# One encoder layer on one core: dense groups of 256 and 272 columns, row sums and squares moved, operands of down loaded ahead, the tail by column groups

## The chip, the core and the metric

The kernel runs on one core of a Trainium2 chip. The metric is the device time of one execution in microseconds (us), the median of three runs. Engines are called as in the profile: PE (TensorE's matmuls), PEld (its weight loads), DVE (VectorE), ACT (ScalarE), POOL (GpSimd) and SP (SyncE, which issues most DMAs here).

## What is computed

One layer of a streaming encoder for 1024 prompt tokens and 32 sample tokens, 1056 columns in all, with a width of 1024 and a hidden width of 4096, in float32:

```
h  = rms_norm(x, ln1_g);   proj = h @ w_in
a  = diff_attention(q, k, v, ...)            # 4 heads, chunk-causal
c  = layer_norm(depthwise_conv(u, w_dw)) ;  c = c * sigmoid(c)
x  = x + concat([a, c]) @ w_out
h2 = rms_norm(x, ln2_g)
x  = x + square(relu(h2 @ w_up)) @ w_down
y  = rms_norm(x, ln_f_g)
```

The other outputs are k, v and the last rows of the convolution's input.

## The kernel before, in words

Tokens are columns: a tile holds 128 features by up to 1056 tokens. Every float32 operand is split into a high part (by ACT, `whi`, `hTh`, `dh`) and a remainder (by DVE or POOL, `wlo`, `hTl`, `dl`), and a product is three matmuls: high by high, low by high, high by low. Instructions stand in the source in one order, and a scheduler arranges each engine's own queue, along which the engine then works.

- **Start and dense blocks** (`x_stat`, `x_group`, `act_groups`, `products`, L101). x is loaded in nine tiles of 128 tokens (the last has 32); `XSET` says which tiles form a set. Per tile, ACT squares and sums it (L262); per set, PE transposes (`pst`), ACT copies (`xT`, L282), DVE scales (`hfx`, L291) and ACT and DVE split into `hTh` (L295) and `hTl` (L296). The blocks of w_in are then multiplied in four groups of columns, `GRP`, 264 each.
- **Out projection** (`part`, then the loop of `pw`, L101). For each of four groups and for the row blocks `ob` 3 to 7, a product is added to x by DVE (L962), and `rows_in` copies x with ln2's gain into the quads `B` (four row blocks of 528 columns), squares it on ACT (L907) and sums the squares on POOL (L908, `ssacc`). Two psum tiles (`psM`) take turns. `b_sums` makes the sums of quads that the up projection needs (`T1`, `T2`, `T4`, L919), for half of the columns at once, all four row blocks.
- **Up projection** (`up_p1`, `up_p2`, `up_steps`). 16 blocks of 256 hidden columns; each is a 2 by 2 block product done with seven products (Strassen-like) from the operands `B00`, `B10` and `X3` to `X7`, the split sums (`to_x`). Five blocks run their first product ahead (`NPRE`), each with one pending psum tile (`psF`, four of two banks). ACT evicts the first product (L1051) and applies relu and square; DVE adds and subtracts (L1067, L1068). The four results and three sums of them go to DRAM (`ud`). `row_stat` makes the mean square of ln2 with a matmul by ones.
- **Down projection** (`u_load`, `u_split`, `d_a`, `w_prep`, `d_run`). Four chunks of the hidden width, each with seven products in the order `PRODS` = 1, 2, 6, 7, 4, 5, 3. A step loads operands two products ahead into pool `act[0]`, splits the next one (`dh` on ACT L876, `dl` on DVE L877), prepares its weights (`w_of` makes sums of them, L1232 to L1235) and adds the result (L1244, or ACT L1281 for the first time). `residual` adds x (kept in DRAM as `x2d`), scaled by `vb` (L1201, L1204), at four places named in `RES`; `row_scales` reads the mean square back for this.
- **Tail** (`final`). Eleven tiles of tokens, `FT`, are transposed back by PE (L1297), squared on ACT (L1302), scaled by DVE (L1303, L1305, L1306) with a power on POOL (L1304), and stored. Five are queued after product 4 of the last chunk, three after half of product 3, three at the end.

## Time and profile before

| | |
|---|---|
| median of three runs | 1224.98 us (1224.97 to 1226.77) |
| the profiled execution | 1224.9 us, its span 1223.1 us |
| mean granted clock | 0.994 |
| PE busy | 1176.2 us, 96% of the span |
| PEld busy | 1131.1 us, 92% |
| DVE busy | 887.9 us, 73% |
| ACT busy | 580.9 us, 47% |
| POOL busy | 142.1 us, 12% |

Busy time is the union of an engine's instructions. A window's row gives, for a stretch of the span, the busy time and number of instructions of each engine and the mean clock that TensorE was granted, as a share of the higher of its levels. A timeline's row gives start, duration, engine, line, operation with the names of its tiles, a count where several are joined, and in brackets how long the engine was idle before and what ended that. Matmuls overlap in the pipeline: one lasts longer than the distance to the next.

### The profile page before, as it was taken

Reading aid. Unit: us, or ns where it says so; the run is one execution under the profiler, and the core shown is the slowest. Engines: PE = TensorE matmul, PEld = TensorE weight load, DVE = VectorE, ACT = ScalarE, POOL = GpSimd, SP = SyncE. Lnnn points to the kernel's source line nnn. Section 1 sums busy time; section 2 is a strip of 40 time slices with the busy share of each in tenths; the row PEclk is TensorE's granted clock in tenths of the full one; section 3 lists DMA queues with packets and bytes.
Section 4 is the critical chain, followed back from the end, with each engine's and each line's share of the span. In section 5 each row is a group of like instructions: output and inputs, shape, how many; then the busy total and the mean of one; then the engine's idle time right before and its main releaser. Section 6 shows DMA issues by size and latency. Waiting matters only on the chain. (4 is left out here: it accounts for less than half of the span.)

```text
span 1223.1 us, 23089 instructions
## 1 busy us (share of the span) xinstructions
PE 1176.2 (96%) x9340; PEld 1131.1 (92%) x9340; DVE 887.9 (73%) x1494; ACT 580.9 (47%) x1160; POOL 142.1 (12%) x149
## 2 busy tenths in 40 slices
PE   6999999999899999989999999999999999999995
PEld 5889988898888789989999999999999999999995
DVE  5797795799975644687776565665865978978865
ACT  7434345433488543665444444444745343333323
POOL 3111122022231221350000000000000000000001
PEclk9999999999999999999999999999999999999998
DMA  6531122122233422234554343445964354454003
GB/s 221 194 101 53 37 66 80 54 62 60 64 110 111 125 89 69 107 97 139 197 190 156 135 152 140 149 142 184 330 225 150 135 188 171 160 193 141 18 23 120
DMA packets 126410, 157.15 MB, mean 128 GB/s; under 512 B 7889, under 2 KB 79458, under 8 KB 126304
## 3 DMA queue, kind: packets, MB, share of 16 engines
q1 hardware_dynamic: 124640, 152.74, 37.3%
q0 software_dynamic: 1664, 2.95, 0.9%
q8 instruction: 73, 1.20, 0.4%
q14 instruction: 33, 0.27, 0.1%
HBM read 104.32 MB, written 51.35 MB: 127 GB/s over the span
## 5 line engine op out<-in xcount | busy, mean ns | idle before, releaser
L987 PE MATMUL pf<-dh,wlo 128*128 128x264 f32 x896 | 144.9, 284 | 2.8 <-DVE wlo L877 2.8
L987 PE MATMUL pf<-dl,whi 128*128 128x264 f32 x896 | 146.9, 286 | 0.0
L987 PE MATMUL pf<-dh,whi 128*128 128x264 f32 x896 | 146.3, 286 | 0.0
L876 ACT ACTIVATE whi<-da 128x512 fp32r<-128x512 f32 x96 | 60.3, 631 | 145.2 <-PE pf L987 141.0
L987 PEld LDWEIGHTS pf<-dh,wlo 128*128 128x128 f32 x896 | 124.1, 189 | 3.0 <-DVE wlo L877 3.0
L987 PEld LDWEIGHTS pf<-dl,whi 128*128 128x128 f32 x896 | 125.0, 189 | 0.0
L987 PEld LDWEIGHTS pf<-dh,whi 128*128 128x128 f32 x896 | 123.4, 189 | 0.1
L101 PE MATMUL pm<-hTh,whi 128*128 128x264 f32 x640 | 107.3, 294 | 6.9 <-ACT tT L347 2.3
L876 ACT ACTIVATE whi<-praw 128x512 fp32r<-128x512 f32 x86 | 53.6, 628 | 107.8 <-PE pf L987 61.6
L78 POOL TENSOR_TENSOR wlo<-raw,whi 128x512 fp32r<-128x512 f32 (+1 forms) x55 | 77.4, 1422 | 229.0 <-PE pm L101 161.0
L101 PE MATMUL pm<-hTh,wlo 128*128 128x264 f32 x640 | 103.8, 287 | 0.0
L101 PE MATMUL pm<-hTl,whi 128*128 128x264 f32 x640 | 102.2, 286 | 1.0 <-DVE hTl L296 1.0
L101 PEld LDWEIGHTS pm<-hTh,whi 128*128 128x128 f32 x640 | 87.2, 188 | 14.0 <-issue 3.2
L101 PEld LDWEIGHTS pm<-hTl,whi 128*128 128x128 f32 x640 | 87.3, 188 | 2.1 <-DVE hTl L296 1.4
L101 PEld LDWEIGHTS pm<-hTh,wlo 128*128 128x128 f32 x640 | 87.8, 188 | 1.3 <-issue 1.3
L1067 DVE TENSOR_TENSOR o<-pf,o 128x528 f32<-128x528 f32 x80 | 56.1, 703 | 44.9 <-PE pf L987 44.7
L1304 POOL TENSOR_TENSOR ssf<-ssf,mhalf 88x1 f32<-88x1 f32 (+2 forms) x11 | 6.0, 547 | 669.4 <-DVE ssf L1303 669.4
L877 DVE TENSOR_TENSOR wlo<-praw,whi 128x512 fp32r<-128x512 f32 x86 | 58.6, 685 | 27.4 <-ACT whi L876 13.4
L877 DVE TENSOR_TENSOR dl<-du,dh 128x2112 fp32r<-128x2112 f32 x28 | 65.9, 2354 | 9.8 <-ACT dh L876 9.4
L1244 DVE TENSOR_TENSOR xa<-pf,xa 128x528 f32<-128x528 f32 (+1 forms) x72 | 48.0, 671 | 34.0 <-PE pf L987 33.9
L877 DVE TENSOR_TENSOR wlo<-da,whi 128x512 fp32r<-128x512 f32 x96 | 64.9, 681 | 10.5 <-ACT whi L876 5.5
L531 ACT ACTIVATE p<-ps,mn 128x128 f32<-128x128 f32 (+6 forms) x64 | 47.4, 742 | 35.2 <-DVE mn L524 30.8
(300 smaller groups left out, 2732.8 us busy)
## 6 DMA issues: line engine op xcount, KB each, us to landing
du<-ud SPq DMA_DIRECT2D x28, 1056.0 KB, 6.0
ud<-o SPq DMA_DIRECT2D x48, 528.0 KB, 3.9
praw<-in_w_up SPq DMA_DIRECT2D x16, 1024.0 KB, 5.5
da<-in_w_down SPq DMA_DIRECT2D x16, 1024.0 KB, 7.5
raw<-in_w_in SPq DMA_DIRECT2D x40, 256.0 KB, 3.0
xTd<-xT SPq DMA_DIRECT2D x8, 528.0 KB, 2.7
x<-xTd SPq DMA_DIRECT2D x8, 528.0 KB
x2d<-x SPq DMA_DIRECT2D x16, 264.0 KB, 2.0
```

Source lines behind the costliest of these rows:

```text
L78: (eng or nc.vector).tensor_tensor(lo[:], raw, hi[:].bitcast(F32), ALU.subtract)
L101: nc.tensor.matmul(out, w[k][a][:, cols], b[k], start=i == 0, stop=i == len(seq) - 1)
L531: nc.scalar.activation(p[:, 0:nk], sc[m], AF.Exp, bias=mn[:, 2 + m : 3 + m], scale=-1.0, accum_out=s0 if m == 0 else s1[:, 0:1],)
L876: nc.scalar.activation(hi, raw, AF.Copy)
L877: nc.vector.tensor_tensor(lo, raw, hi.bitcast(F32), ALU.subtract)
L987: nc.tensor.matmul(out, wi[:, k, :], bj[:, k, GW * hb : GW * hb + GW], start=first and n == 0, stop=n == len(seq) - 1, skip_group_check=no ...
L1067: add = lambda o, ps, b: nc.vector.tensor_tensor(halves(o), ps, halves(b), ALU.add)
L1244: nc.vector.tensor_tensor(o, ps, o, ALU.add)
L1304: nc.gpsimd.tensor_tensor(ss, ss, mhalf[:n, 0:1], ALU.pow)
```

## The change

It consists of six parts. (1) The dense groups are 256, 272, 272 and 256 columns, x's sets are 2, 3, 2 and 2 tiles (tile 2 is loaded behind the first block of w_in), and the squares of tiles 0 and 1 go from ACT to DVE. (2) The squares and sums for ln2 leave `rows_in`; down reads x back from DRAM at four steps (`SQR`), ACT squares it, DVE sums it into `vb`, and `row_stat` and `row_scales` follow at step (1, 6); the residuals move to later steps. (3) `b_sums` works for some row blocks at a time, within the loop of the out projection; some quads lie in the other pool. (4) Two first products may be pending in up. (5) The first operands of down are loaded (and one split) before the last two blocks of up, and those blocks keep `o3` in a quad instead of a transpose buffer. (6) Products 5 and 3 of the last chunk run together, for columns 0 to 272 and then 272 to 528; the final tiles are ten.

```diff
-GRP = tuple((GW * g, GW) for g in range(4))
+GRP = ((0, 256), (256, 272), (528, 272), (800, 256))
-XSET = ((0, 1, 2), (3, 4), (5, 6), (7, 8))
+XSET = ((0, 1), (2, 3, 4), (5, 6), (7, 8))
...
-        nc.scalar.activation(ac[:n, j % 4, 0:D], xts[j][:n], AF.Square, accum_out=ss[:n])
+        if j < 2:
+            nc.vector.tensor_tensor_reduce(
+                ac[:n, j % 4, 0:D], xts[j][:n], xts[j][:n], 1.0, 0.0, ALU.mult, ALU.add, ss[:n]
+            )
+        else:
+            nc.scalar.activation(ac[:n, j % 4, 0:D], xts[j][:n], AF.Square, accum_out=ss[:n])
...
     def rows_in(ob, c0, n):
         xs = x2[ob][:, c0 : c0 + n]
-        if ob == 0:
-            nc.scalar.activation(ssacc[:, c0 : c0 + n], xs, AF.Square)
-        else:
-            sq = sqp.tile([P, GW], F32, tag="sq", name="sq2")[:, 0:n]
-            nc.scalar.activation(sq, xs, AF.Square)
-            nc.gpsimd.tensor_tensor(ssacc[:, c0 : c0 + n], ssacc[:, c0 : c0 + n], sq, ALU.add)
...
-    def b_sums(g):
-        s = slice(GW * g, GW * g + GW)
-        sub = lambda o, a, b: nc.vector.tensor_tensor(o[:, :, s], a, b, ALU.subtract)
-        if g == 0:
+    def b_sums(g, which, k0, n):
+        if not T:
             for i in (1, 2, 4):
-                T[i] = quad(act[0], f"T{i}")
-        sub(T[1], B[0][1][:, :, s], B[0][0][:, :, s])
-        sub(T[2], B[1][1][:, :, s], T[1][:, :, s])
-        sub(B[0][1], B[1][1][:, :, s], B[0][1][:, :, s])
-        sub(T[4], B[1][0][:, :, s], T[2][:, :, s])
+                T[i] = quad(act[i // 4], f"T{i}")
+        s = slice(GRP[g][0] - HT, GRP[g][0] - HT + GRP[g][1])
+        k = slice(k0, k0 + n)
+        sub = lambda o, a, b: nc.vector.tensor_tensor(o[:, k, s], a[:, k, s], b[:, k, s], ALU.subtract)
+        if 1 in which:
+            sub(T[1], B[0][1], B[0][0])
+        if 2 in which:
+            sub(T[2], B[1][1], T[1])
+            sub(B[0][1], B[1][1], B[0][1])
+            sub(T[4], B[1][0], T[2])
...
+    SUMS = {3: [((1,), 0, 4)], 5: [((2,), 0, 2)], 6: [((2,), 2, 1)], 7: [((2,), 3, 1)]}
...
             rows_in(ob, c0, w)
+            if g > 1 and ob in SUMS:
+                for a in SUMS[ob]:
+                    b_sums(g, *a)
...
-            b_sums(0)
...
-        t3 = tTp.tile([P, HT], F32, tag="tT", name="o3")
+        t3 = o3q[:, 2 * (p % 2), :] if p >= NP_ - 2 else tTp.tile([P, HT], F32, tag="tT", name="o3")[:]
...
-    pend1 = None
+    pend = deque()
     for p in range(NPRE):
         ps = up_p1(p)
-        if pend1:
-            up_p2(*pend1)
-        pend1 = p, ps
+        pend.append((p, ps))
+        if len(pend) > 2:
+            up_p2(*pend.popleft())
         if p == 0:
-            b_sums(1)
...
-    up_p2(*pend1)
-    row_stat()
+    while pend:
+        up_p2(*pend.popleft())
...
     last = [NP_ - 2, NP_ - 1]
+    o3q = quad(q2, "o3q")
+    u_load(0, 1, q2)
+    u_split(0, 1)
+    u_load(0, 2, q2)
...
-    FT = [(P * j, P) for j in range(4)] + [(4 * P, HT - 4 * P)] + [(HT + 88 * j, 88) for j in range(6)]
+    FT = [(P * j, P) for j in range(4)] + [(4 * P, HT - 4 * P)]
+    FT += [(HT, 91), (HT + 91, 91), (HT + 182, 90), (HT + 272, P), (HT + 400, P)]
...
+    def squares(kh, th):
+        x = xq.pop((kh, th))
+        v = vb[:, HT * th : HT * th + HT]
+        nc.scalar.activation(x[:], x[:], AF.Square)
+        nc.vector.tensor_tensor(x[:, 0:2, :], x[:, 0:2, :], x[:, 2:4, :], ALU.add)
+        if kh:
+            nc.vector.tensor_tensor(v, v, x[:, 0, :], ALU.add)
+            nc.vector.tensor_tensor(v, v, x[:, 1, :], ALU.add)
+        else:
+            nc.vector.tensor_tensor(v, x[:, 0, :], x[:, 1, :], ALU.add)
...
+    LAST = ((0, 272, (5, 6, 7)), (272, 256, (8, 9)))
...
+        if end and i == 5:
+            last5[:] = w, u
+            return
         if end and i == 3:
-            for hb in range(2):
-                for m in range(4):
-                    if m % 2 == 0:
-                        ps = acc_tile()
-                    mm1(ps[:, m % 2, 0:GW], w[m], u, hb, True)
-                    add(ACC[5][m][:, GW * hb : GW * hb + GW], ps[:, m % 2, 0:GW])
-                    fin_step()
-                if hb == 0:
-                    fin.extend([lambda: None] + [lambda j=j: final(j) for j in range(5, 8)])
+            for c0, n, tiles in LAST:
+                for a, wu in ((4, last5), (5, (w, u))):
+                    for m in range(4):
+                        if a == 4 and m % 2 == 0:
+                            held[m] = held[m + 1] = acc_tile()
+                        ps = held[m][:, m % 2, 0:n]
+                        mm1(ps, wu[0][m], wu[1], c0, n, a == 4)
+                        add(ACC[a][m][:, c0 : c0 + n], ps)
+                        fin_step()
+                fin.extend([lambda j=j: final(j) for j in tiles])
             return
...
-    RES = {(1, 2): (0, 0), (1, 4): (1, 0), (2, 2): (0, 1), (2, 4): (1, 1)}
+    SQR = {(0, 6): (0, 0), (0, 4): (1, 0), (0, 3): (0, 1), (1, 2): (1, 1)}
+    STAT = 1, 6
+    RES = {(1, 5): (0, 0), (2, 2): (1, 0), (2, 4): (0, 1), (2, 3): (1, 1)}
...
-        if (c, i) == (0, 3):
-            row_scales()
+        if (c, i) in SQR:
+            residual_load(*SQR[c, i])
...
         d_run(c, i, w)
+        if (c, i) in SQR:
+            squares(*SQR[c, i])
+        if (c, i) == STAT:
+            row_stat()
+            row_scales()
```

Three places where the order of an engine's queue moves:

DVE at the end of the out projection, before (x<-pw are the adds that free a psum tile, T and B<-B the sums, 128x4x264 is four row blocks):

```order
L962 TENSOR_TENSOR x_5005<-pw,x_5005 128x264
L919 TENSOR_TENSOR T_6502<-B_6076,T_6501 128x4x264
L919 TENSOR_TENSOR B_6074<-B_6076,B_6074 128x4x264
L962 TENSOR_TENSOR x_5077<-pw,x_5077 128x264
L877 TENSOR_TENSOR wlo<-wraw,whi 128x512
L962 TENSOR_TENSOR x_5085<-pw,x_5085 128x264
L919 TENSOR_TENSOR T_6501<-B_6074,B_6073 128x4x264
L919 TENSOR_TENSOR T_6503<-B_6075,T_6502 128x4x264
```

The same place now:

```order
L965 TENSOR_TENSOR x_5077<-pw,x_5077 128x256
L880 TENSOR_TENSOR wlo<-wraw,whi 128x512
L921 TENSOR_TENSOR T_6340<-B_6070,B_6069 128x4x256
L965 TENSOR_TENSOR x_5085<-pw,x_5085 128x256
L880 TENSOR_TENSOR wlo<-wraw,whi 128x512
L921 TENSOR_TENSOR T_6341<-B_6072,T_6340 128x2x256
L921 TENSOR_TENSOR B_6070<-B_6072,B_6070 128x2x256
L965 TENSOR_TENSOR x_5931<-pw,x_5931 128x256
```

The sums of four row blocks between two adds are cut into pieces of two and one, and only T1 is still done for four.

DVE at the switch from up to down, before (o<-o are the last subtractions of up, da<-da and ds the sums of down's weights):

```order
L1233 TENSOR_TENSOR da<-ds_10570,da 128x4x512
L1068 TENSOR_TENSOR o_10076<-o_10076,o_10077 128x528
L877 TENSOR_TENSOR dl<-du,dh 128x2112
L1068 TENSOR_TENSOR o_10323<-o_10076,o_10046 128x528
L1234 TENSOR_TENSOR da<-da 128x4x512
L1235 TENSOR_TENSOR da<-da 128x4x512
L877 TENSOR_TENSOR dl<-du,dh 128x2112
L877 TENSOR_TENSOR wlo<-da,whi 128x512 x3
L1068 TENSOR_TENSOR o_10077<-o_10077,o_10323 128x528
```

The same place now:

```order
L1257 TENSOR_TENSOR da<-ds_10478,da 128x4x512
L880 TENSOR_TENSOR wlo<-da,whi 128x512
L1072 TENSOR_TENSOR o_9995<-pf,o_9994 128x528
L880 TENSOR_TENSOR dl<-du,dh 128x2112
L1073 TENSOR_TENSOR o_9964<-o_9995,o_9964 128x528
L880 TENSOR_TENSOR wlo<-da,whi 128x512
L1073 TENSOR_TENSOR o_9966<-o_9966,o_9967 128x528
L1258 TENSOR_TENSOR da<-da 128x4x512
L880 TENSOR_TENSOR wlo<-da,whi 128x512
```

The weight sums no longer stand side by side: a wlo lies between them, and one dl fewer stands here.

PE at the end of the program, before (pf are matmuls, pfin the transposes of the final tiles):

```order
L1297 MATMUL pfin<-cst,xa 88x128 x9
L987 MATMUL pf<-dh,whi 128x264 x4
L987 MATMUL pf<-dl,whi 128x264 x4
L987 MATMUL pf<-dh,wlo 128x264 x4
L1297 MATMUL pfin<-cst,xa 88x128 x32
```

The same place now:

```order
L1325 MATMUL pfin<-cst,xa 128x128 x9
L992 MATMUL pf<-dh,whi 128x256 x4
L992 MATMUL pf<-dl,whi 128x256 x4
L992 MATMUL pf<-dh,wlo 128x256 x4
L1325 MATMUL pfin<-cst,xa 128x128 x4
```

Of the final transposes, 4 rather than 32 stand behind the last matmul.

## Rows read from the trace of the kernel before

**Rows 1.** Windows, cut at the stages: start:end, us, busy (x instructions) per engine, clock, DMA, GB/s
```profile
0.00:30.60 30.60, 19.78 (x126) 17.41 (x127) 16.91 (x46) 24.01 (x60) 11.49 (x25) 1.00 0.68 221
30.60:520.20 489.60, 473.12 (x3646) 433.76 (x3646) 364.06 (x788) 241.45 (x636) 106.68 (x98) 1.00 0.28 86
520.20:550.80 30.60, 26.24 (x199) 25.60 (x197) 24.54 (x23) 20.98 (x36) 17.93 (x17) 0.94 0.31 97
550.80:887.40 336.60, 336.60 (x2748) 335.04 (x2747) 228.11 (x334) 167.14 (x270) 0.00 (x0) 1.00 0.51 174
887.40:918.00 30.60, 27.78 (x217) 27.57 (x217) 20.02 (x22) 13.39 (x20) 0.00 (x0) 0.94 0.68 230
918.00:1193.40 275.40, 275.40 (x2273) 275.40 (x2273) 218.04 (x252) 104.43 (x128) 1.53 (x3) 1.00 0.38 131
1193.40:1224.00 30.60, 17.29 (x144) 16.28 (x142) 16.17 (x34) 9.51 (x16) 4.49 (x9) 0.87 0.34 108
```

**Rows 2.** Timeline of the start: start us, us, engine, line, operation, idle before
```profile
10.17 1.06 ACT L262 ACTIVATE ac<-xt 128x1024 f32<-128x1024 f32 x1
...
11.23 0.61 ACT L76 ACTIVATE whi<-raw 128x512 fp32r<-128x512 f32 x1
...
13.01 0.87 ACT L282 ACTIVATE xT<-pst 128x384 f32<-128x384 f32 x2
...
15.38 0.51 PE L101 MATMUL pm<-hTh,whi 128*128 128x264 f32 x2 [0.34 <-ACT hTh L295]
```

**Rows 3.** Timeline of the end of the out projection
```profile
526.11 0.41 PE L101 MATMUL pw<-cath,wboth 128*128 128x264 f32 x2
...
527.42 1.79 DVE L919 TENSOR_TENSOR B<-B,B 128x1056 f32<-128x1056 f32 x1
...
529.61 2.02 PE L101 MATMUL pw<-cath,whi 128*128 128x264 f32 x8 [3.08 <-DVE x L962]
...
533.18 1.02 PE L101 MATMUL pw<-cath,wlo 128*128 128x264 f32 x7
```

**Rows 4.** Timeline of the beginning of up
```profile
544.26 1.25 DVE L919 TENSOR_TENSOR T<-B,T 128x1056 f32<-128x1056 f32 x1
...
546.09 1.97 ACT L876 ACTIVATE X7h<-B 128x2112 fp32r<-128x2112 f32 x1
...
546.24 0.75 PE L987 MATMUL pf<-B10h,whi 128*128 128x264 f32 x4 [1.24 <-ACT o L1051]
```

**Rows 5.** Timeline of the first products of down
```profile
888.46 0.65 PE L987 MATMUL pf<-dl,whi 128*128 128x264 f32 x4
...
888.91 2.35 DVE L877 TENSOR_TENSOR dl<-du,dh 128x2112 fp32r<-128x2112 f32 x1
...
891.92 1.25 PE L987 MATMUL pf<-dh,wlo 128*128 128x264 f32 x4 [2.82 <-DVE wlo L877]
...
895.81 0.65 PE L987 MATMUL pf<-dh,whi 128*128 128x264 f32 x4
```

**Rows 6.** Windows: the third chunk of down
```profile
1038.60:1119.60 81.00, 81.00 (x670) 81.00 (x669) 69.02 (x78) 30.18 (x36) 0.00 (x0) 1.00 0.50 173
```

**Rows 7.** Groups by line and shape: DVE's residual in the third chunk of down
```profile
L1204 DVE TENSOR_TENSOR xa<-xa,xq 128x528 f32<-128x528 f32 x8 | 5.6, 696 | 0.0
...
L1201 DVE TENSOR_TENSOR xq<-xq,vb 128x2112 f32<-128x2112 f32 x1 | 2.4, 2359 | 0.4 <-DMA xq<-x2d 0.4
```

**Rows 8.** Timeline of the tail
```profile
1206.17 0.65 PE L987 MATMUL pf<-dh,wlo 128*128 128x264 f32 x4
...
1208.09 0.42 DVE L1244 TENSOR_TENSOR xa<-pf,xa 128x264 f32<-128x264 f32 x1
...
1208.23 1.95 PE L1297 MATMUL pfin<-cst,xa 128*88 128x128 f32 x16 [0.53 <-DVE y L1306]
...
1215.47 1.28 DVE L1306 SCALAR_TENSOR_TENSOR y<-pfin,ssf,lnfb 88x1024 f32<-88x1024 f32 x1
...
1217.72 1.28 DVE L1306 SCALAR_TENSOR_TENSOR y<-pfin,ssf,lnfb 88x1024 f32<-88x1024 f32 x1
```

86 lines of the change are left out of this document (39 added, 47 removed).

## Prediction

> **What bounds the kernel now.** I read the windows first, cut where the stages end. TensorE (PE) is busy without a gap in two long stretches, 550.8 to 887.4 and 918.0 to 1193.4: there only fewer or shorter matmuls could save time, and the change brings neither. What PE loses lies in five places [rows 1]: 10.8 us at the start, 16.5 us scattered over 30.6 to 520.2, 4.4 us in the slice from 520.2, 2.8 us in the slice from 887.4, and 13.3 us in the last slice. In both short slices the mean granted clock is 0.94 instead of 1.00, so the loss is larger than the idle time. For those places I then read the timeline, row by row, to see which instruction PE stood behind and what its engine was doing in place of it. The profiled execution took 1224.9 us, 1.8 us more than its span and 0.08 us less than the median of the runs; the sum is made against it.
>
> **A matmul's price.** 275.4 us hold 2273 recorded matmuls of mostly 264 columns [rows 1]: 121 ns each. Sixteen transposes of 128 columns take 1.95 us [rows 8], 0.11 each when the last one's own end is taken off.
>
> **Start: x in sets of two tiles, two squares on DVE, groups of 256 and 272.** Before, ScalarE (ACT) does the squares of three tiles, 1.06 us each, ahead of the first weight conversion at 11.23, and the first dense matmul starts at 15.38 [rows 2]. The edit takes two squares (2.1 us) from ACT, but puts all eight xT copies of set 0 and the square of tile 2 ahead of the first hTh. In the new order, with the durations of these rows: four conversions of 0.61 (2.4), eight xT copies of 256 columns (two of 384 take 0.87, so two of 256 at least 0.58: 2.3 to 2.8), one square 1.06, a first hTh 0.4 like an xT copy, together 6.2 to 6.7. From 11.2 that is 17.4 to 17.9, about 2.3 later. Against it, group 0 is complete with two tiles rather than three: one tile's four copies, 0.43 each, and its share of hTh and hTl no longer stand ahead of its last matmuls, 1.7 us on ACT alone. What counts is when PE stops waiting, so I take +0.6. Bounds: -2.1 (the two squares simply vanish) and +2.3 (the later start stays).
>
> **Groups of 256 and 272 elsewhere.** About 2690 matmuls of the dense blocks and of the out projection, and 192 of the last two products of down, are half 256 and half 272 columns wide. Between 128 and 264 columns a matmul grows from 111 to 121 ns. If it grows evenly around 264, the sum is unchanged: I take 0. If only one half changes its price, and in full proportion (8 x 121 / 264 = 3.7 ns), it is 1440 x 3.7 ns = 5.3 us, either way.
>
> **Out projection to up: the sums by row blocks.** Before, the DVE add that frees the psum of the product stands behind 128x1056 subtractions, the last of 1.79 us; PE is idle 3.08 us at 529.61 and then runs at the lower of its two clock levels: 16 matmuls, from 526.5 to 533.18, take 6.68 instead of 1.93 us, 4.75 lost [rows 3]. In the new order the work between two such adds is at most a wlo and two subtractions of 2 x 256 columns, which I put at 0.70 each like an add of 528 columns [rows 7]: 2.1 us. The product has two psum tiles, and one product of 24 matmuls lasts 2.9 us, which covers that. If the cover is gone, PE loses what the piece takes, not 3 us. So -4.75. The 28 squares on ACT and 28 adds on GpSimd vanish here too; 1.79 against 1.25 us for a subtraction of the same size after GpSimd has gone quiet [rows 3, 4] says the rest of DVE's work gets shorter.
>
> Then the new wait: ACT's eviction of the first product already stands behind one conversion of 1.97 us, and PE waits 1.24 for it [rows 4]. In the new order X6h and X7h both stand ahead of it, and X3h ahead of a later one; against that two first products may be pending. From ACT's durations I place the first eviction 1.0 us and the later one 1.0 us behind PE: 2.0 instead of 1.24, +0.8. Bounds: -1.24 (the second pending product covers all), +4.7 (an idle stretch of 3 us with the slow clock behind it, as in rows 3). Together **-3.9**, between -6.0 and 0.
>
> **Up to down: operands ahead.** Before, DVE does the last adds of up, two operand sums and dl of 2.35 us ahead of three wlo; PE stops 2.82 us at 891.92 and is at half clock afterwards: 24 matmuls from 888.46 to 895.81 take 7.35 instead of 2.90 us, 4.45 lost [rows 5]. Now the first operand is split before the last two blocks of up, dl is gone from in front of those wlo, and o3 no longer waits for a transpose buffer that ACT's eviction stood behind. The work taken off DVE there is 2.35 us, and the sums stand apart with wlo between them; counting the durations of the new order from the first product of down, I find the wlo about 8 us ahead of its use. **-4.4**, between -4.5 and 0. The loads that SP takes ahead (1056 KB each) go under the last blocks of up, with no PE idle.
>
> **Squares in down.** ACT gets four squares of 128x2112, 1.97 us each [rows 4]; it is busy 30 of 81 us in the third chunk of down [rows 6], so nothing. DVE gets four adds of 128x1056 (1.25 [rows 4]) and six of 128x528 (0.70 [rows 7]): 9.2 us over two chunks. The residuals move later: the third chunk gets three. Before, DVE is busy 69.0 of 81.0 us there with one multiplication and eight adds of the residual, 8.0 us; without them 61.0, with three residuals of 2.35 + 4 x 0.70 = 5.15 it is 76.5 of 81.0. That fits, so 0, but it is the narrowest place. The row statistic's matmuls move and cost the same. Behind them stands a chain: store, read back, ten small reads on SP, and one operand load of down behind these on SP. The operand has the whole step before its use, 96 x 0.121 = 11.6 us, to come in; the trace of before shows no such wait. Bounds: 0 and +4.5 (a stall like that of rows 5).
>
> **Tail.** Before, the last L987 matmul ends at 1206.8, 32 transposes come after it, and the final tiles follow each other 2.25 us apart on DVE and ACT; the last scaling ends at 1219.0 and the span 4.1 later, 16.3 us after PE's last product [rows 8]. Now four transposes are left there, and all but the last two tiles are normalised before. Chain after the last product at T: add 0.42, transposes 0.5, then from the first transpose's end to the end of the scaling what a final tile takes for its square, the small steps and the scaling, which I put at 3.8 (three steps of some 1.25 each), that is T + 4.7 for the first; the second 2.3 later, as the tiles follow now; 4.1 to the end: T + 11.1. T itself comes 20 transposes later, 2.2 us. Net 16.3 - 11.1 - 2.2 = **-3.0**, between -4.5 and 0 (a tile that waits for the accumulators).
>
> **Scattered waits**, 30.6 to 520.2: the order shifts with the groups; 0, within 3 us either way.
>
> **Sum**: 0.6 - 3.9 - 4.4 - 3.0 = -10.7. 1224.9 - 10.7 = 1214.2, and 0.1 to the median: **1214.3 us**.
>
> **A rule weighed.** At 546.24 PE waits 1.24 us for a psum tile and its next four matmuls take 0.75 us, about what four take at the higher level (0.65) and not the 1.25 of the lower one [rows 4, 5]: a wait of this size did not cost the clock. The Trainium skill, "TensorE: Matmul & The Clock Gate", section "A second HAM failure mode: psum-queue depth-cycling", says that PE's small idle times between groups of matmuls that cycle through psum banks can make the clock swing between its levels. By the rows, the two evictions in up that are 1 us late cost 2.0 us. By that rule they bring stretches at the lower level too, which is rival 3.
>
> **Rivals.**
> (1) One of the four repairs leaves a stall behind: an eviction in up, or an operand of down. Price 4.5 us, as twice in this trace. For it: the new ACT order in up, and DVE at 76.5 of 81.0 us. Against it: the 8 us of margin at the start of down, the step of 11.6 us for each operand. 1218.8 us. Chance 0.20.
> (2) A matmul of 256 columns keeps the price of 264 and 272 pays 3.7 ns more: +5.3, 1219.6 us. Against it: a transpose of 128 columns is 10 ns cheaper, so 264 does not sit on a floor. Chance 0.05.
> (3) The two late evictions in up each bring the lower clock level. In rows 3 it took 4.75 - 3.08 = 1.7 us beyond the idle time; twice that is 3.4, 1217.7 us. Against it: [rows 4]. Chance 0.04.
> (4) Slower: DVE falls behind in the third chunk of down. Three residuals at products 2, 4 and 3 lie within its seven steps; a step lasts 96 x 0.121 = 11.6 us and DVE needs 61.0 / 7 + 5.15 = 13.9 in each such step, 2.3 too much, so the weights come later where they were not prepared far enough ahead. Each stall costs 4.5 us with the slow clock behind it [rows 5]; from the third on the gain is gone: 1214.3 + 13.5 = 1227.8 us. For it: DVE at 69.0 of 81.0 us there already. Against it: the steps between have room (8.7 of 11.6). Chance 0.09.
> (5) It does what it says at one of the two stage borders only, and start and down give back the rest: 1222.5 to 1225. About no change. Chance 0.07.
>
> **How the numbers follow.** My forecast has 0.55. The forecast's own range, with the start, the eviction and the scattered waits at half their bounds, is 1210 to 1218. Rivals 1 to 3 (0.29) lie at 1217.7 to 1219.6 with a few us on either side, so the range of 8 in 10 runs from 1209.0 to 1221.5. A measurement of this kernel can tell 0.2%, 2.45 us, from no change. Below 1222.5 lie the forecast and rivals 1 to 3: faster 0.84; rival 5: same 0.07; rival 4: slower 0.09.
>
> **What would show it.** In the changed profile: no PE wait of 3 us for a DVE add of the out projection, and clock 1.00 through the first 30 us of up; no wait for wlo at the first products of down; four transposes after the last product and about 11 us from there to the end; DVE at 75 or more of 81 us in the third chunk with PE still whole. I am wrong if a dip of the clock shows at either border, if PE idles in the second or third chunk of down, if the dense stretches hold fewer matmuls per us, or if the first dense block ends more than 2 us later.

## The result, and the profile after

| | before | changed |
|---|---|---|
| median | 1224.97 us (4 runs, 1221.71 to 1226.77) | 1217.86 us (4 runs, 1217.14 to 1218.14) |
| ratio of the two | | 0.9927 [0.9901, 0.9953] |
| profiled execution, its span | 1224.9, 1223.1 us | 1217.83, 1216.1 us |
| granted clock | 0.994 | 0.992 |

The changed kernel is faster by 0.7%, 7.1 us of the 10.7 that were forecast. The time lies within the range, on its slow side.

The windows of the changed kernel, with the cuts and columns of [rows 1]:

```profile
0.00:30.60 30.60, 22.79 (x142) 21.11 (x143) 17.88 (x52) 21.83 (x57) 10.27 (x23) 1.00 0.67 221
30.60:520.20 489.60, 475.42 (x3617) 432.71 (x3617) 361.51 (x785) 236.71 (x618) 101.62 (x87) 0.99 0.28 86
520.20:550.80 30.60, 28.60 (x220) 28.16 (x219) 24.47 (x39) 16.66 (x23) 0.00 (x0) 0.94 0.35 109
550.80:887.40 336.60, 336.60 (x2758) 336.60 (x2757) 230.34 (x334) 171.72 (x274) 0.00 (x0) 1.00 0.51 174
887.40:918.00 30.60, 30.60 (x251) 30.60 (x251) 23.27 (x26) 16.57 (x21) 0.00 (x0) 1.00 0.85 308
918.00:1193.40 275.40, 275.27 (x2256) 273.47 (x2254) 221.66 (x265) 105.82 (x127) 2.75 (x5) 1.00 0.40 141
1193.40:1217.00 23.60, 12.06 (x100) 11.37 (x99) 10.69 (x23) 5.79 (x10) 2.74 (x5) 0.80 0.28 92
```

The slice from 887.4 is whole now, at full clock. The slice from 520.2 still has a clock of 0.94: the stall of the out projection is gone, and another one, in up, has come into the same slice. The stretch from 30.6 has more busy time and yet fewer matmuls than before, at 0.99: it has lost something that busy time alone doesn't show.

Windows move against the work when a stage grows shorter, so I also cut each trace at the work itself. The marks are four rows of the timeline: the first matmul of the dense blocks, of the out projection, of down, and the row statistic that now stands in down:

```profile
14.25 0.78 PE L102 MATMUL pm<-hTh,whi 128*128 128x256 f32 x2
...
501.20 0.48 PE L102 MATMUL pw<-cath,wboth 128*128 128x256 f32 x2
...
865.98 0.65 PE L992 MATMUL pf<-dh,whi 128*128 128x264 f32 x4
...
983.93 1.94 PE L1214 MATMUL pf<-vb,ones 128*1 128x264 f32 x8
```

Two marks in up lie between them: its first product, and the first product with X6, where the pending first products end. The table has, for each kernel of this study, the time from mark to mark, in us; the tail runs from the end of the last product to the end of the span. The stage "heads" holds the row statistic (1.94 us) in before and e_sq, "down" holds it in all others.

| kernel | first dense matmul at | dense and attention | out projection | heads of up | rest of up | down | tail |
|---|---|---|---|---|---|---|---|
| before | 15.38 | 484.21 | 37.49 | 33.23 | 299.00 | 337.52 | 16.3 |
| changed | 14.25 | 486.95 | 32.89 | 32.86 | 299.02 | 338.85 | 11.2 |
| e_start | 15.85 | 483.59 | 32.83 | 30.95 | 299.12 | 338.85 | 11.2 |
| e_grp264 | 21.84 | 478.76 | 32.81 | 31.76 | 299.07 | 338.83 | 11.2 |
| e_sums | 15.31 | 486.28 | 34.49 | 29.20 | 298.88 | 338.85 | 11.2 |
| e_sq | 13.38 | 485.87 | 34.95 | 37.22 | 299.10 | 338.88 | 11.5 |
| e_pend1 | 13.40 | 486.89 | 32.82 | 35.80 | 298.97 | 338.83 | 11.2 |
| e_x2 | 13.30 | 487.20 | 32.82 | 30.90 | 299.70 | 338.83 | 11.2 |
| e_ops | 13.84 | 486.63 | 32.81 | 33.90 | 299.11 | 338.76 | 11.2 |
| e_o3 | 14.95 | 487.29 | 32.81 | 31.15 | 299.80 | 345.07 | 11.2 |
| e_opso3 | 14.46 | 486.68 | 32.85 | 32.13 | 299.76 | 349.14 | 11.2 |
| e_tail | 15.06 | 487.81 | 32.78 | 31.18 | 299.98 | 336.24 | 16.1 |
| c_sx | 13.32 | 483.46 | 32.83 | 30.38 | 299.66 | 338.83 | 11.2 |
| c_sxr | 12.95 | 482.73 | 32.82 | 29.98 | 299.87 | 337.58 | 11.2 |

Each row is one execution. Where an edit does not reach a stage, the stage keeps its length to some tenths of a us in out projection, down and tail, to 1.1 us in rest of up, to 2 us in dense and attention and to 3 us in heads of up (30.95 in e_start, 33.90 in e_ops). A small effect is therefore read from its stage and not from the whole time, whose ratios have intervals of 0.002 to 0.005; in the heads of up an effect below 3 us is not shown by one pair of rows. From before to changed the columns give -1.13 + 2.74 - 4.60 - 0.37 + 0.02 + 1.33 - 5.1 = -7.1; the spans give -7.0.

**Start** (timeline, PE), before and changed:

```profile
8.92 0.69 PE L276 MATMUL pst<-cst,xt 128*128 128x128 f32 x2 [3.29 <-DMA xt<-in_x_prompt]
```

```profile
6.88 1.54 PE L282 MATMUL pst<-cst,xt 128*128 128x128 f32 x6 [1.25 <-DMA xt<-in_x_prompt]
```

PE waits for a tile of x that landed 2.0 us sooner in this execution of the changed kernel. In the kernels of the table this moment lies between 6.4 and 9.3 us, with the old sets and with the new ones (9.33 in e_start, 6.44 in c_sxr, 8.79 in e_sums, 6.78 in e_sq). From there to the first dense matmul it is 6.5 us in before and 7.4 in changed. So the 1.1 us by which the first matmul came earlier go with a landing that scatters, and are not shown to be the edit's. PE's first dense matmuls in the changed kernel also run at the lower level (0.41 us each up to 19.7, 0.28 in before).

**End of the out projection** in the changed kernel (timeline, PE and one row of DVE):

```profile
520.89 1.17 PE L102 MATMUL pw<-catl,whi 128*128 128x272 f32 x8
...
528.35 1.21 PE L102 MATMUL pw<-cath,whi 128*128 128x256 f32 x8
...
528.81 1.22 DVE L921 TENSOR_TENSOR T<-B,B 128x1024 f32<-128x1024 f32 x1
```

No idle time stands in brackets, and eight matmuls take 1.2 where they took 2.02 at the lower level [rows 3]. DVE's subtraction of 1024 columns takes 1.22, the one of 1056 took 1.79 at this place before.

**Beginning of up** (timeline, ACT and PE):

```profile
542.43 1.95 ACT L879 ACTIVATE X7h<-B 128x2112 fp32r<-128x2112 f32 x1
...
544.28 0.59 ACT L1056 ACTIVATE o<-pf 128x528 f32<-128x528 f32 x1
...
544.92 0.80 PE L992 MATMUL pf<-B10h,whi 128*128 128x264 f32 x4 [1.94 <-ACT o L1056]
...
545.52 1.08 PE L992 MATMUL pf<-B10l,whi 128*128 128x264 f32 x4
...
546.40 1.08 PE L992 MATMUL pf<-B10h,wlo 128*128 128x264 f32 x4
```

One eviction is late, by 1.94 us, behind the conversion that makes X7h. Then four matmuls take 1.08 us rather than 0.65: the clock falls to its lower level, which it had not done behind the 1.24 us of [rows 4].

**Tail** (timeline, PE and DVE), against [rows 8]:

```profile
1204.19 0.63 PE L992 MATMUL pf<-dh,wlo 128*128 128x256 f32 x4
1204.66 0.38 PE L1325 MATMUL pfin<-cst,xa 128*128 128x128 f32 x2
...
1205.34 0.44 PE L1325 MATMUL pfin<-cst,xa 128*128 128x128 f32 x2 [0.30 <-DVE xa L1268]
...
1208.01 1.28 DVE L1334 SCALAR_TENSOR_TENSOR y<-pfin,ssf,lnfb 128x1024 f32<-128x1024 f32 x1
...
1210.28 1.28 DVE L1334 SCALAR_TENSOR_TENSOR y<-pfin,ssf,lnfb 128x1024 f32<-128x1024 f32 x1
```

Four transposes and two scalings are left behind the last product.

### The profile page after: what moved, and what is told of

The parts are those of the page before. It is cut to its first block, busy times and chain, and to the rows that moved or that the text cites. A ratio compares the mean times of both kernels' runs of the same rounds, so it can differ in the third digit from the quotient of the medians.

```text
span 1216.1 us, 23002 instructions
## 1 busy us (share of the span) xinstructions
PE 1181.3 (97%) x9332; PEld 1134.0 (93%) x9332; DVE 889.8 (73%) x1517; ACT 575.1 (47%) x1126; POOL 117.4 (10%) x120
## 4 chain that ended last, share of the span: by engine, by line
PE 82%; DVE 11%; ACT 1%; issue 1%; DMA 1%; ACTq 0%; POOL 0%; POOLq 0%; DVEq 0%
PE pf L992 53%; PE pm L102 17%; DVE ac L440 3%; PE ps L521 3%; PE pw L102 2%; DVE ac L446 2%; DVE ac L453 2%; PE po L558 2%; PE pat L554 1%; PE pfin L1325 1%; PE pss L643 1%; DMA wraw<-in_w_up 1%; DVE ps L530 0%; DVE p L544 0%; PE pso L699 0%
## 5 line engine op out<-in xcount | busy, mean ns | idle before, releaser
L992 PE MATMUL pf<-dh,whi 128*128 128x264 f32 (+2 forms) x896 | 146.6, 286 | 0.0
L992 PE MATMUL pf<-dl,whi 128*128 128x264 f32 (+2 forms) x896 | 146.3, 285 | 0.0
L992 PE MATMUL pf<-dh,wlo 128*128 128x264 f32 (+2 forms) x896 | 144.8, 283 | 0.0
L102 PE MATMUL pm<-hTh,whi 128*128 128x256 f32 (+1 forms) x640 | 107.6, 295 | 4.2 <-ACT tT L353 2.1
L102 PE MATMUL pm<-hTh,wlo 128*128 128x256 f32 (+1 forms) x640 | 106.0, 291 | 0.0
L102 PE MATMUL pm<-hTl,whi 128*128 128x256 f32 (+1 forms) x640 | 105.7, 291 | 0.0
L79 POOL TENSOR_TENSOR wlo<-raw,whi 128x512 fp32r<-128x512 f32 (+1 forms) x55 | 80.3, 1475 | 236.3 <-PE pm L102 140.9
L102 PEld LDWEIGHTS pm<-hTl,whi 128*128 128x128 f32 x640 | 89.9, 193 | 1.6 <-issue 1.3
L1332 POOL TENSOR_TENSOR ssf<-ssf,mhalf 128x1 f32<-128x1 f32 (+3 forms) x10 | 5.5, 548 | 716.8 <-DVE ssf L1331 716.8
L1268 DVE TENSOR_TENSOR xa<-pf,xa 128x528 f32<-128x528 f32 (+2 forms) x72 | 46.2, 642 | 32.9 <-PE pf L992 32.3
```

The costliest lines, as they stand in the source:

```text
L79: (eng or nc.vector).tensor_tensor(lo[:], raw, hi[:].bitcast(F32), ALU.subtract)
L102: nc.tensor.matmul(out, w[k][a][:, cols], b[k], start=i == 0, stop=i == len(seq) - 1)
L992: nc.tensor.matmul(out, wi[:, k, :], bj[:, k, c0 : c0 + n], start=first and i == 0, stop=i == len(seq) - 1, skip_group_check=not first,)
L1268: nc.vector.tensor_tensor(o, ps, o, ALU.add)
```

## The experiments

All start from the changed kernel, except the two c_ kernels, which combine edits. Each edit makes the scheduler arrange the queues anew, so waits and falls of the clock move in stages that the edit does not touch.

### The start: groups and sets

Two kernels undo part 1 of the change: e_start wholly, e_grp264 only the widths of the groups.

```diff
-GRP = ((0, 256), (256, 272), (528, 272), (800, 256))
+GRP = tuple((GW * g, GW) for g in range(4))
```

and in e_start as well

```diff
-XSET = ((0, 1), (2, 3, 4), (5, 6), (7, 8))
+XSET = ((0, 1, 2), (3, 4), (5, 6), (7, 8))
...
-        if j < 2:
+        if j < 0:
...
+    x_load(2)
```

> The changed kernel with the start and the dense groups as before: four groups of 264 columns, x in sets of 3, 2, 2 and 2 tiles, all squares of x on ACT, tile 2 loaded early. Theory: between the first dense matmul and the out projection the changed kernel loses 2.7 us, because the clock falls twice (at 74.5 and 292.9 us), each time behind a wait of PE of 1.6 us for the attention's kql; with the old groups these waits are at most 1.5 us and the clock stays at its higher level, so the out projection starts about 1.6 us earlier (499.6 rather than 501.2) and the time falls to about 1216.3 us. Rival A: the groups are not the cause, the falls stay with any order of the other parts: 1217.9 us. Rival B: the earlier first dense matmul of the change (14.25 rather than 15.38) is worth its 1.1 us and is lost: 1219 us.

> The changed kernel with only the four groups of columns back at 264; x's sets, the squares of x on DVE and everything else as changed. With start and groups both undone the time was 1213.8 us and the stretch from the first dense matmul to the out projection 483.6 us, against 487.0 in the changed kernel. Theory: the groups' widths (by the order that follows from them) cost these 3.4 us, and x's new sets keep the earlier first dense matmul: the stretch is 483.6 again, and in the new order the first eviction of up stands ahead of X7h, so the wait of 1.94 us there is gone too: about 1212.8 us. Rival: x's sets and the squares on DVE cost them: the stretch stays at 487, only up's wait goes: 1214.4 us.

Measured: e_start 1213.81 us (1211.53 to 1214.5), 0.9898 [0.9881, 0.9915] of the kernel before. Its slowest run lies 2.6 us below the changed kernel's fastest (1217.14), but the intervals of the two ratios overlap. Its stretch up to the out projection is 3.4 us shorter (483.59 against 486.95), while its first matmul comes 1.6 us later: 1.8 net. Another 1.9 comes in the heads of up, where its late eviction costs PE 0.62 us instead of 1.94; that is within the scatter of that stage. e_start took 2.5 us less than expected. e_grp264: 1215.54 us, 0.9909 [0.9891, 0.9926]; it begins 7.6 us later than the changed kernel, catches up 8.2, and reaches the out projection at 500.60 instead of 501.20. So the moment of the first matmul decided nothing here. Neither the theory (1212.8 us) nor the rival had this: the wait for up's eviction stayed, at 0.96 us.

The price of a width can be read directly. From the starts of neighbouring matmuls in the dense blocks and the out projection (distances under 135 ns), the mean distance is 117.7 ns for 256 columns and 125.6 for 272 in the changed kernel, and 121.8 for 264 in the one before: linear, so 256 and 272 together cost twice 264 to 0.3 ns. The loss is thus in the order and not in the columns. The stretch took 485.9 to 487.8 us in all nine kernels that have widths and sets as changed, and 482.7 to 484.2 in the four that have both as before; this, and not one pair of times, shows that part 1 costs time. In the changed kernel some of it shows as waits, such as this one of PE, behind which the clock falls:

```profile
291.66 0.50 PE L521 MATMUL ps<-kql,kqh 64*128 64x128 f32 x4 [1.64 <-DVE kql L366]
```

But a fall is not the whole cause: e_start has two (at 75.5 and 311.0) and is short all the same. Cut at matmuls that stand in both timelines (behind PE's waits near 73, 292 and 311 us), the changed kernel is 0.4, 0.4, 1.3 and 1.3 us longer than e_start in the four pieces: the last 1.3 lie behind 311 us, where it has no fall and e_start has one. Which step of the order costs it stays open.

### The out projection: row sums or squares

e_sums makes the sums of all four row blocks behind row block 7; e_sq puts the squares, GpSimd's adds, the row statistic and the residuals back to where they were.

```diff
-    SUMS = {3: [((1,), 0, 4)], 5: [((2,), 0, 2)], 6: [((2,), 2, 1)], 7: [((2,), 3, 1)]}
+    SUMS = {7: [((1, 2), 0, 4)]}
```

```diff
         xs = x2[ob][:, c0 : c0 + n]
+        if ob == 0:
+            nc.scalar.activation(ssacc[:, c0 : c0 + n], xs, AF.Square)
+        else:
...
+            nc.scalar.activation(sq, xs, AF.Square)
+            nc.gpsimd.tensor_tensor(ssacc[:, c0 : c0 + n], ssacc[:, c0 : c0 + n], sq, ALU.add)
...
-    RES = {(1, 5): (0, 0), (2, 2): (1, 0), (2, 4): (0, 1), (2, 3): (1, 1)}
+    RES = {(1, 2): (0, 0), (1, 4): (1, 0), (2, 2): (0, 1), (2, 4): (1, 1)}
```

> The changed kernel with the sums of up's operands for all four row blocks at once, behind row block 7 of groups 2 and 3. Theory: DVE adds of the out projection stand behind two subtractions of 1.3 us each again; with two psum tiles a wait of PE of 1.5 to 3 us comes back and the clock falls: the out projection takes 35.5 to 37.5 us rather than 32.9: 1220.5 to 1222.5 us. Rival A: without the squares' adds on GpSimd the subtractions take 1.25 rather than 1.8 us each, which the psum tiles cover: 1217.9 us. Rival B: a wait below 1.5 us, without a fall: 1219 us.

> The changed kernel with the squares for the row statistic as before: on ACT and GpSimd in the out projection, the statistic in up, the residuals at their earlier steps. Theory: the squares in down cost PE nothing (it is whole there) and their removal from the out projection is worth only what the shorter subtractions bring: DVE's pieces take 0.6 rather than 0.43 us and the adds come later, but within the cover of two psum tiles: 1217 to 1219 us. Rival A: the POOL adds are what held DVE: out projection 35 us or more, 1220 us or more. Rival B: the pace of down is faster from early on, because the statistic's matmuls or a wait come earlier: 1216.5 us.

Measured: e_sums 1216.02 us, 0.9909 [0.9892, 0.9927]; e_sq 1224.85 us, 0.9986 [0.9975, 0.9997]. Both theories missed: e_sums lies below all three of its expectations, e_sq where its rival A put it. The cut of the sums is worth 1.6 us in its own stage (34.49 against 32.89). In the next one e_sums is shorter (heads 29.20 against 32.86), as the late eviction of the changed kernel does not occur there; whether the sums cause that or the new arrangement is open, and in the whole time the two kernels' intervals overlap. The squares are worth 2.1 us in the out projection, 2.4 in the heads (37.22 - 1.94 against 32.86, less than that stage's scatter), and 7.2 us of the median in all (0.9986 - 0.9927 of 1225 us). The profiled execution of e_sq is the fastest of its twelve and 4.8 us longer than that of the changed kernel, so 2.4 of the 7.2 are in no trace. Neither alone brings back the stall of 3.08 us of [rows 3]; both undone together were not run. What remains in e_sums at that place, and in e_sq (timelines, PE):

```profile
530.33 1.21 PE L102 MATMUL pw<-cath,whi 128*128 128x256 f32 x8 [1.73 <-DVE x L965]
```

```profile
528.46 1.21 PE L102 MATMUL pw<-cath,whi 128*128 128x256 f32 x8 [1.15 <-DVE x L974]
...
547.24 0.76 PE L1001 MATMUL pf<-B10h,whi 128*128 128x264 f32 x4 [3.34 <-ACT o L1065]
```

Why the squares matter here is seen in DVE's own rows. First the subtractions of e_sq, where GpSimd works beside them (L974 adds from psum), then those of the changed kernel, where it is quiet:

```profile
524.21 1.00 DVE L930 TENSOR_TENSOR B<-B,B 128x272 f32<-128x272 f32 x1
...
527.64 0.43 DVE L930 TENSOR_TENSOR B<-B,B 128x272 f32<-128x272 f32 x1
527.99 0.41 DVE L974 TENSOR_TENSOR x<-pw,x 128x256 f32<-128x256 f32 x1
...
531.23 1.07 DVE L930 TENSOR_TENSOR T<-B,T 128x512 f32<-128x512 f32 x1
```

```profile
524.87 0.44 DVE L921 TENSOR_TENSOR B<-B,B 128x272 f32<-128x272 f32 x1
...
532.58 0.68 DVE L921 TENSOR_TENSOR T<-B,T 128x512 f32<-128x512 f32 x1
```

With GpSimd's adds around, a subtraction of 272 columns takes 0.43 or 1.00 us, without them 0.44; one of 512 takes 1.07 against 0.68. The adds from psum take 0.41 to 0.44 in both kernels. The Trainium skill, "GPSIMD Engine Reference", section "1. Specifications", says that GpSimd shares its SBUF interfaces with VectorE and gets in the way of VectorE's instructions with two SBUF inputs. These rows agree, and the adds with a psum input are spared. The edit also brings ACT's squares back, and DVE then waits for ACT's copies of x (1.20 us ahead of 523.85 and 0.85 ahead of 526.75 in e_sq, 0.59 ahead of 524.51 in the changed kernel); how much of the 2.1 us is GpSimd's and how much ACT's was not tried apart.

### The heads of up: one or two pending products, and the conversions

e_pend1 goes back to one pending product. e_x2 keeps two, and makes ACT do each of the conversions of X3 to X7 in two halves, between which an eviction can stand.

```diff
-        if len(pend) > 2:
+        if len(pend) > 1:
```

```diff
...
+        for k in range(0, 4, 2):
+            nc.scalar.activation(hi[:, k : k + 2, :], raw[:, k : k + 2, :], AF.Copy)
...
```

> The changed kernel with one pending first product in up rather than two. Theory: PE's wait of 1.94 us is for a psum tile behind the first eviction, which stands behind X7h on ACT whatever is pending; the number of pending products moves nothing there: 1217.9 us within 0.5, the same wait and the same fall of the clock. Rival A: two pending products are what makes PE ask for the tile sooner than the eviction comes (a second first product before the second products of the first): with one the wait shrinks to the 1.24 us of before and the clock holds: 1215.5 us. Rival B: the second pending product covers ACT's conversions: with one the wait grows to 3 us: 1219 us.

> The changed kernel with ACT's conversions X3h to X7h each in two halves of 128x1056 instead of one of 128x2112. Theory: the first eviction of up then stands behind X6h only; PE waits at most 0.3 us for it instead of 1.94 and the clock does not fall at 545 us: 1.9 + 1.7 = 3.5 us less, 1214.4 us. Rival A: the wait only moves to the second eviction, behind X7h and X5h: PE waits about 1 us there, 1216.5 us. Rival B: ACT was late for the eviction's input and not by the conversion: 1217.9 us.

Measured: e_pend1 1219.44 us, 0.9951 [0.993, 0.9972]; e_x2 1215.26 us, 0.9914 [0.9899, 0.9928]. e_pend1 came out as its rival B said, e_x2 near its theory. With one pending product PE waits 4.00 us (and the heads take 2.9 us longer):

```profile
544.88 1.25 PE L992 MATMUL pf<-B10h,whi 128*128 128x264 f32 x4 [4.00 <-ACT o L1056]
```

With halves the eviction comes ahead of X7h, and the largest wait that is left there is 0.42 us for a weight:

```profile
539.93 0.59 ACT L1056 ACTIVATE o<-pf 128x528 f32<-128x528 f32 x1
540.42 2.05 ACT L1112 ACTIVATE X7h<-B 128x1056 fp32r<-128x1056 f32 x2
...
546.00 0.76 PE L992 MATMUL pf<-B00h,whi 128*128 128x264 f32 x4 [0.42 <-ACT whi L879]
```

The heads are 2.0 us shorter than in the changed kernel, but no shorter than in some kernels with whole conversions (30.95 in e_start, 31.15 in e_o3), so the wait tells more than the length. With whole conversions PE's wait for that eviction is never the same twice: none in e_sums, 0.62 us in e_start, 0.96 in e_grp264, 1.24 in before, 1.49 in e_o3, 1.50 in e_tail, 1.94 in the changed kernel, 2.33 in e_opso3, 2.77 in e_ops, 3.34 in e_sq, 4.00 in e_pend1; in all three kernels with halves (e_x2, c_sx, c_sxr) it is not there. So the halves take the wait away, and e_sums shows that they are not the only way. The wait in e_pend1, with one pending product, is the longest, but before has one as well, and with two the wait scatters by 3.3 us, so what the second one is worth is not told by this one run.

### Up to down: operands ahead, and where o3 lies

Part 5 has two halves. e_ops undoes the loads and the split ahead and keeps `o3` in a quad; e_o3 undoes only the quad; e_opso3 undoes both.

```diff
-    u_load(0, 1, q2)
-    u_split(0, 1)
-    u_load(0, 2, q2)
...
+    u_split(*seq[0])
```

```diff
...
-        t3 = o3q[:, 2 * (p % 2), :] if p >= NP_ - 2 else tTp.tile([P, HT], F32, tag="tT", name="o3")[:]
+        t3 = tTp.tile([P, HT], F32, tag="tT", name="o3")[:]
```

> The changed kernel with the operands of down loaded and split at down's start as before (o3 stays in its quad). Theory: DVE has the first dl in front of the first weights again; PE idles 2 to 3 us about 20 us after the first product of down, the clock falls, 4.4 us lost; behind the stall a matmul of down takes 121.4 ns rather than 122.8, which gives back up to 1.1 us over the next 100 us. So 1221.2 to 1222.3 us. Rival A: o3 in its own quad is what removed the stall, not the early split: 1217.9 us. Rival B: only the idle time comes back, without the fall of the clock: 1220 us.

> The changed kernel with the operands of down loaded and split at down's start AND o3 of the last two blocks back in a transpose buffer, as before. With the operands alone undone nothing changed in down. Theory: o3's own quad (ACT's first evictions of down no longer behind it) is what removes the stall: PE idles 2 to 3 us some 20 us after the first product of down and the clock falls, 4.4 us, partly given back by the faster pace of 121.4 ns behind a stall: 1220.5 to 1222.3 us. Rival: neither is needed, since the order of DVE's weight sums alone has changed: 1217.9 us.

> The changed kernel with only o3 of the last two blocks of up back in a transpose buffer; the operands of down stay loaded and split ahead. The operands alone undone cost nothing in down; both undone cost 10.3 us there, with PE idle 8.7 us behind ACT's first eviction of down. Theory: o3's quad alone removes the stall, because ACT's first eviction into a2 has to wait for the transpose buffers that o3 holds until DVE's last subtraction, and in ACT's queue the weights' conversions stand behind that eviction: PE idles 6 us or more at the start of down, 1224 us or more. Rival: each of the two edits suffices alone, since with the operands split early DVE reaches that last subtraction 4.7 us sooner: at most a wait of 4 us, 1218 to 1222 us.

Measured: e_ops 1218.01 us, 0.9936 [0.9921, 0.9952], down 338.76 like the changed kernel's 338.85: loading the operands ahead is worth nothing that can be seen, as its rival A said. e_opso3 1228.03 us, 1.0012 [1.0, 1.0024], down 349.14, 10.3 longer, more than either expectation. e_o3 1222.12 us, 0.9963 [0.9948, 0.9979], down 345.07, 6.2 longer, between theory and rival. In e_o3 (ACT and PE) the stall comes right behind the first product of down, from 877.8 on, and is for an eviction, not a wlo:

```profile
881.75 1.11 ACT L1311 ACTIVATE a<-pf 128x528 f32<-128x528 f32 x2 [1.90 <-DVE o L1073]
...
882.42 1.11 PE L992 MATMUL pf<-dh,whi 128*128 128x264 f32 x4 [4.61 <-ACT a L1311]
```

In e_opso3 the same eviction stands behind a square of down, which waits for its DMA:

```profile
882.93 1.96 ACT L1196 ACTIVATE xq<-xq 128x2112 f32<-128x2112 f32 x1 [3.08 <-DMA xq<-x2d]
...
885.84 1.09 ACT L1308 ACTIVATE a<-pf 128x528 f32<-128x528 f32 x2
...
886.49 1.25 PE L992 MATMUL pf<-dh,whi 128*128 128x264 f32 x4 [8.67 <-ACT a L1308]
```

So the changed kernel needs the quad for `o3` at this border; with it the operands come early enough from their old place. The stall of before at 891.92 for wlo [rows 5] comes back in none of the three. What removed it is shown in part only. In e_ops DVE again does a dl and two weight sums side by side ahead of a wlo, and PE waits for none (timeline, DVE):

```profile
880.34 2.35 DVE L880 TENSOR_TENSOR dl<-du,dh 128x2112 fp32r<-128x2112 f32 x1
882.61 2.28 DVE L1255 TENSOR_TENSOR da<-da 128x2048 f32<-128x2048 f32 x1
884.81 2.28 DVE L1256 TENSOR_TENSOR da<-da 128x2048 f32<-128x2048 f32 x1
887.02 0.68 DVE L880 TENSOR_TENSOR wlo<-da,whi 128x512 fp32r<-128x512 f32 x1
```

DVE is 7.8 us without a wlo there, 12.3 in before ahead of 891.18. So with the quad in place neither the split made ahead nor the distance between these two sums is needed. In before, ACT also sat idle for 5.41 us, for one of the last subtractions of up, ahead of an eviction of down:

```profile
893.72 1.11 ACT L1281 ACTIVATE a<-pf 128x528 f32<-128x528 f32 x2 [5.41 <-DVE o L1068]
```

That is the wait which the quad is for, but PE's stall of before ended with a wlo 1.8 us earlier. The quad alone in the kernel before, and the whole new order of sums and wlo undone alone, were not run.

### The tail

e_tail puts `LAST`, the ten tiles and the products 5 and 3 back as they were.

```diff
-    FT = [(P * j, P) for j in range(4)] + [(4 * P, HT - 4 * P)]
-    FT += [(HT, 91), (HT + 91, 91), (HT + 182, 90), (HT + 272, P), (HT + 400, P)]
+    FT = [(P * j, P) for j in range(4)] + [(4 * P, HT - 4 * P)] + [(HT + 88 * j, 88) for j in range(6)]
...
+    for j in range(8, 11):
+        final(j)
```

> The changed kernel with the tail as before: products 5 and 3 of the last chunk apart, eleven final tiles of which three stand at the end. Theory: from the last product to the end 16.3 us instead of 11.3, with 20 transposes fewer before it (2.2 us): 2.8 us more, 1220.7 us. Rival A: the whole 5.0 us, 1222.9 us (the transposes before the last product cost nothing). Rival B: no difference, 1217.9 us.

Measured: 1219.97 us, 0.9951 [0.9936, 0.9965], near the theory; tail 16.1 instead of 11.2, down 336.24 instead of 338.85, net 2.2 us for the new tail in these stages (2.9 in the ratios, whose intervals overlap). The last two scalings on DVE start 2.25 us apart, at 1211.69 and 1213.94, as before.

### Together: a version that beats both

c_sx has the old start of e_start and the halves of e_x2. c_sxr adds one matmul of a single column ahead of the first X6 product and of the first product of down, to see whether the distance between matmuls hangs on something that such a matmul sets (below).

```diff
...
+            if (c, i, m) == (0, 1, 0):
+                nc.tensor.matmul(ps[0:1, 1, 500:501], ones[:], ones[:], start=True, stop=True)
             v = mm(ps, w[m], u, not second)
```

> The changed kernel with start and groups as before (264 columns, x in sets of 3, 2, 2, 2, all squares of x on ACT) and with the conversions X3h to X7h in halves. Theory: start and groups undone gave 1213.8 us with 63.8 us from the first product of the out projection to the first X6 product; waits of 0.62 and 0.56 us for the eviction and for a weight are left there, and both are behind a whole conversion of 1.97 us on ACT or DVE: with halves 0.6 to 1.2 us less, 1212.9 us. Rival: ACT only waits for the weights' DMA there and the halves gain nothing: 1213.8 us.

> As the kernel before it in this call, and a matmul of one column by one column of ones ahead of the first X6 product of up and of the first product of down, into a part of the psum tile that nothing reads. Theory: the distance between matmuls is a state of TensorE's queue, 122.8 ns at the start of down and 121.4 behind the row statistic's matmuls or behind a stall; a small float32 matmul with a weight of one column sets the faster state as the row statistic's four do: down takes 121.4 ns from its start, 1.1 us less over its first 115 us, and up's 122.0 may fall as well: 1 to 2 us less, 1211.5 us. Rival A: the state is set by a wait of PE and not by these matmuls: 122.8 ns stays until the row statistic, 0.1 us more, 1213.0 us. Rival B: it is set by the position of the instructions in their stream: the distance changes, but not necessarily to 121.4.

Measured: c_sx 1212.15 us (1211.2 to 1215.24), 0.9892 [0.9871, 0.9913]; c_sxr 1210.77 us (1208.94 to 1216.04), 0.9883 [0.9858, 0.9907]. Both are near their expectations. Their slowest runs lie below the changed kernel's fastest, though the intervals of the ratios touch its lower end; the two are not told apart. In the stages, c_sx adds the gain of the halves only in part (heads 30.38 against 30.95), since in e_start the wait is 0.62 to begin with. c_sxr's down is 1.25 us shorter than that of c_sx; its small matmul and what follows:

```profile
858.23 0.19 PE L1315 MATMUL pf<-ones 128*1 128x1 f32 x2
858.35 0.76 PE L993 MATMUL pf<-dh,whi 128*128 128x264 f32 x4
...
975.08 1.94 PE L1222 MATMUL pf<-vb,ones 128*1 128x264 f32 x8
```

From the first product of down to the row statistic it is 116.73 us, in the changed kernel 117.95 for the same matmuls. In the profiled execution of c_sxr the clock does not fall between the first dense matmul and the tail; in the changed kernel it falls three times.

## Why the prediction was right in sign and too large

**Start, widths and scattered waits** (forecast +0.6, 0 and 0): measured -1.1 + 2.7 = +1.6. The widths alone are priced rightly at 0, and rival 2 did not happen. The step that failed is the later first matmul, by 2.3 us, and what was set against it: counted from the landing of x it came 0.9 us later, the earlier landing was luck, and the stage still ended later than before. The order behind the start was taken at 0 within 3 us; it costs 3.4 against e_start and was never worked out.

**Out projection to up** (-4.75): measured -4.6, the right size. The step on the cause was half right. It named the cut of the sums; undoing that costs 1.6 us, undoing the squares 2.1. The squares' leaving was mentioned there and priced at nothing of its own; with them back the subtractions are long, 1.07 against 0.68 us.

**The new wait** (+0.8, two evictions 1.0 late each): measured +1.6 without the row statistic (32.86 against 33.23 - 1.94). It is one eviction, late by 1.94, and a fall of the clock behind it. Rival 3 happened for one of its two evictions. That this term came out near its price is luck: the same wait lies anywhere between 0 and 3.34 us in the kernels with two pending products, and the stage scatters by 3 us. By the prediction's own list a dip of the clock at either border, and fewer matmuls per us in the dense stretches, were to show it wrong; both are there (0.94 in the slice from 520.2, 3617 against 3646 matmuls in the same 489.6 us). The Trainium skill, "TensorE: Matmul & The Clock Gate", section "A second HAM failure mode: psum-queue depth-cycling", says that frequent small idle times between groups of matmuls that cycle through psum make the clock swing. The traces agree in part: one such wait of 1.94 us was followed by a fall at 545.5, one of 1.24 [rows 4] and one of 2.33 (e_opso3) were not.

**Up to down** (-4.4): the window from 887.4 is whole at clock 1.00, where 2.8 us were idle and 4.45 lost. The size is right and the step on the cause is not borne out: it counted the dl taken away and the sums set apart. Taking the split back costs nothing (e_ops, with two sums side by side again), taking the quad of `o3` back costs 6.2 us. The quad stood in the prediction's sentence as a third reason without a price. Which part removed the stall of before stays open.

**Squares in down** (0): DVE was the narrowest place in the forecast, at 76.5 of 81.0 us, and rival 4 rested on it. The third chunk of the changed kernel, to be read against [rows 6]:

```profile
1032.30:1113.80 81.50, 81.50 (x674) 81.50 (x673) 73.55 (x83) 30.73 (x35) 0.00 (x0) 1.00 0.51 178
```

DVE is busy 73.55 of 81.50 and PE without a gap: rival 4 did not happen, nor did a stall in down (rival 1). DVE stays 3 us below its forecast. Down takes 338.85; from before one expects 337.52 - 4.45 (stall) + 1.94 (row statistic) + 2.2 (20 transposes) = 337.2. Of the 1.6 too much, some 1.1 is a slower pace (95 us at 122.8 ns rather than 121.4): between the first product of down and the row statistic the matmuls of 264 columns stand 122.8 ns apart, behind it 121.4. In before the same change of pace comes some 22 us into down, behind the stall at 891.92. The squares are not shown to cost anything: without them down takes 338.88 in e_sq, where it lacks the row statistic as well. The forecast had one price of 121 ns for all matmuls [rows 1].

**Tail** (-3.0): from 16.3 to 11.2, forecast 11.1; less 20 transposes of 2.2 us together that is -2.9, and e_tail gives 2.2 by its stages and 2.9 by the ratios. Right.

The missing 3.6 us are thus the order behind the start (1.0), the late eviction with its clock (0.8), down and mostly its pace (1.6), and the out projection and the tail (0.2). None is one of the repairs failing: the expected gains came, and small terms that had been put at 0 or too low took a third of them back.

## What to carry to other kernels

Undo the parts of a change one by one even where it won: groups of 256 and 272 with their sets cost more than they brought, operands ahead did nothing that can be seen, and undoing the squares alone takes back nearly the whole gain. Know first how far a stage moves that the edit does not touch: here up to 3 us. A long conversion on ACT ahead of an eviction was worth cutting in two: PE waited for the eviction in ten of eleven kernels with whole conversions and in none of three with halves. A first matmul that starts earlier is no gain until the end of its stage has moved.
